# Splitting the gate weights of a forgetting attention in quarters, at fixed places of two engines' order

## The chip, the core and the metric

The kernel runs on one core of a Trainium2 chip. The core has five engines that each work through their own list of instructions in order and wait for each other by semaphores: TensorE (PE in the profile; PEld is its loading of weights), VectorE (DVE), ScalarE (ACT), GpSimd (POOL) and SyncE (SP), which only issues DMAs here. The metric is the device time of one launch in microseconds (us).

## The reference

One DeepNorm layer over a sequence of 1024 frames with 1024 channels, in float32: a forgetting attention with 16 heads of 64, then a SwiGLU with 2816 channels. Both are modulated by a conditioning vector. What matters here is the attention with its output gate:

```python
def fox_mixer(h, w_in, b_f, q_g, k_g, w_o):
    proj = h @ w_in
    q, k, v, f_logit, o = jnp.split(proj, [D, 2 * D, 3 * D, 3 * D + N_HEADS], axis=-1)
    ...
    y = fox_block_attention(q, k, v, F)     # causal softmax(q k^T * scale + F_q - F_k) v, per head
    y = y.transpose(0, 2, 1, 3).reshape(B, T, D)
    return (y * jax.nn.sigmoid(o)) @ w_o
```

The gate `o` is one more projection of `h`, 1024 columns wide.

## The kernel before

Float32 products are made from high and low parts: an operand x is cast on ScalarE to a rounded type (`xh`), VectorE subtracts that from x (`xl`), and TensorE sums `xh*yh + xl*yh + xh*yl`. The kernel first projects q, k and v for all frames and stores them in DRAM, then runs the attention head by head, then the output projection and the SwiGLU.

The attention works in pairs of heads (`pr`, 8 of them). For a head, `scores` makes the products of q and k (L535, L536; tile `s`) in six steps into two PSUM buffers of two banks each. VectorE adds the causal mask to the diagonal block (L540) and takes the row maximum (L542, `nm`), ScalarE makes the exponential (L543, `p`). A buffer is free again once its exponential has been made. `values` transposes `p` on TensorE (L596, `t`), casts it (L601, `ph`), subtracts (L602, `pl`) and multiplies it with the values (L579, L580; `o`). At the end of a half of the rows, ScalarE copies one half of `o` (L585, `yt`) and VectorE adds the other (L586, `y`). GpSimd multiplies `y` by the gate and the inverse row sums (`lb`, from a small DRAM round trip): `sg` (L636), then `lb*sg` (L657) and `y*lb` (L659), the last as soon as `y` is there.

`gates` is a generator that fills TensorE's stream: for each pair and each half of the rows it makes 24 products (8 blocks of the contraction, 3 products each, L631, bank `og`), and the tanh (L635) after the 24th. `GC` says how many of these products each of the 12 steps of a head takes. Their weights are 128 columns for a pair. `gate_raw` loads them (512 KB, tile `wor`, one buffer), and `gate_weights` splits them in two parts of 4 blocks each: a cast of 512 elements a partition (L614, `woh`) and a subtraction (L615, `wol`). Part 0 of the next pair is made while the current pair's second half runs, at its block 5, right after the load is issued; part 1 is made when the next pair begins. The same buffer `wor` takes the first weights of the output projection (`wo100r`) after the last pair.

The kernel is written through a tile layer that lists instructions in program order and then reorders each engine's list, by what it expects to be ready. `tc.keep_in_program_order(i)` holds instruction i behind everything that was written before it on its engine. The kernel before uses it only in the SwiGLU. Heads are written one step ahead: all scores of head 0 come first, then 12 steps, each with some gate products, a step of the next head's scores, and a step of this head's values.

Of the kernel before, what the change touches and what calls it, by code (L numbers as in the profile page):

```python
# [9 lines left out]
F32R = mybir.dt.float32r  # L10
BF16 = mybir.dt.bfloat16
AF = mybir.ActivationFunctionType
ALU = mybir.AluOpType
# [3 lines left out]
P = 128  # L17
# [7 lines left out]
NP = H // 2  # L25
# [10 lines left out]
def f32(ap):  # L36
    return ap.bitcast(F32)
# [8 lines left out]
def fox_trunk_kernel(  # L46
# [17 lines left out]
    nc = tc.nc  # L64
# [3 lines left out]
    wo = fox_w_o[0]  # L68
# [28 lines left out]
    def bank(tag, name):  # L97
        return ps.tile([P, 512], F32, name=name, tag=tag, bufs=3 if tag == "T" else 1)
# [150 lines left out]
    for kt in range(KT):  # L249
# [9 lines left out]
        wh, wl = w0[kt // 2]  # L259
# [227 lines left out]
    gws = {}  # L487

    def gate_raw(pr):
        raw = ld[0].tile([P, KT, P], F32, name=f"wor{pr}", tag="owr", bufs=1)  # L490
        nc.sync.dma_start(raw, win[:, 3 * D + H + pr * P:3 * D + H + (pr + 1) * P]
                          .rearrange("(k p) e -> p k e", p=P))
        gws[pr] = [raw]
# [19 lines left out]
    pv_cm.__exit__(None, None, None)  # L513
    wt_cm.__exit__(None, None, None)


    yp = ctx.enter_context(tc.tile_pool(name="yp", bufs=1, side="right", reuse_waits="tile"))
    y32 = yp.tile([P, NP, T], F32, name="y32")
# [2 lines left out]
    def right(name):  # L521
        cm = tc.tile_pool(name=name, bufs=1, side="right", reuse_waits="tile")
        at_cms.append(cm)
        return cm.__enter__()

    a_o, ld1, a_p, a_t, at = [right(f"at_{n}") for n in "olptx"]
# [79 lines left out]
                wait.append((product, (hf, kbk, c0, ph, pl)))  # L606
                yield

    def gate_weights(pr, part):

        raw = gws[pr][0][:, part * 4:part * 4 + 4, :]
        wh = a_o.tile([P, 4, P], F32R, name=f"woh{pr}{part}", tag=f"owh{part}", bufs=1)
        wl = a_o.tile([P, 4, P], F32R, name=f"wol{pr}{part}", tag=f"owl{part}", bufs=1)
        nc.scalar.copy(wh, raw)  # L614
        nc.vector.tensor_tensor(wl, raw, f32(wh), ALU.subtract)  # L615
        gws[pr].append((wh, wl))

    def gates():

        gate_weights(0, 0)  # L620
        for pr in range(NP):
            gate_weights(pr, 1)
            for hf in HALVES:
                a = bank("T", f"og{pr}_{hf}")
                for kt in range(KT):
                    if hf == HB and kt == 5 and pr + 1 < NP:
                        gate_raw(pr + 1)
                        gate_weights(pr + 1, 0)
                    wh, wl = gws[pr][1 + kt // 4]
                    for n, (l, r) in enumerate(((wh, hTh), (wl, hTh), (wh, hTl))):  # L630
                        nc.tensor.matmul(a, l[:, kt % 4, :], r[hf][:, kt, :], start=(kt == 0 and n == 0),  # L631
                                         stop=(kt == KT - 1 and n == 2))
                        if kt == KT - 1 and n == 2:
                            sg = at.tile([P, 512], F32, name=f"sg{pr}_{hf}", tag="sg", bufs=2)
                            nc.scalar.activation(sg, a, AF.Tanh, scale=0.5)  # L635
                            nc.gpsimd.tensor_scalar(sg, sg, 0.5, 0.5, op0=ALU.mult, op1=ALU.add)  # L636
                            sgs[pr, hf] = sg
                        yield
# [24 lines left out]
    HA, HB = HALVES  # L663
# [35 lines left out]
    def start(h):  # L699
# [4 lines left out]
        return tl, probs, scores(h, tl, state[pr][0], probs)  # L704

    sgs, gg = {}, gates()
    cur, wait = start(0), []
    run(cur[2], 12)
    for h in range(H):
        pr = h // 2  # L710
        nxt = start(h + 1) if h + 1 < H else None
        v = values(h, cur[0], cur[1])
        for step in range(12):
            if h % 2 and step in (1, 5):
                hf = HALVES[step == 5]
# [162 lines left out]
    for hf in HALVES:  # L878
# [8 lines left out]
        for cc in range(4):  # L887
# [5 lines left out]
            for i in range(4):  # L893
                tt = hf * 4 + i
                a = out_bank(i, f"wa{tt}_{cc}")[:, 0:256]
                for kt in range(KT):
                    wh, wl = w[kt // 4]
# [75 lines left out]
        return others  # L973

    banks, fds = {}, []
    keep = tc.keep_in_program_order

    def open_bank(tag, ff, n):
        banks[tag, ff] = psA.tile([P, 512], F32, name=f"{tag}{ff}", tag=tag, bufs=n)
# [324 lines left out]
```

## Time and profile before

| what | us |
|---|---|
| median of 3 runs | 1408.03 (1404.87 to 1409.60) |
| the profiled execution | 1409.46, its span 1407.7 |
| TensorE busy | 1354.5 (96%) |
| VectorE busy | 1025.7 (73%) |
| ScalarE busy | 584.6 (42%) |
| GpSimd busy | 343.5 (24%) |
| attention, first score product to last value product | 342.7 to about 649 |

The span runs from the first to the last instruction. A busy time is the union of an engine's instructions; matmuls are pipelined, so two that follow each other overlap in the rows, and the distance of their starts is what one costs. PEclk is TensorE's granted clock as a share of its full 2.4 GHz. A note in brackets at the end of a row is the time in which the engine sat idle before it, and the instruction that ended this. The mean granted clock of this execution was 0.992.

### The profile page before, as it was taken

What the parts mean: (1) busy time and instruction counts of PE and PEld (TensorE: products, weight loads), DVE (VectorE), ACT (ScalarE), POOL (GpSimd) and SP (SyncE); (2) the same over time, 40 slices, a digit from 0 to 9 for tenths busy, and PEclk for the clock granted to TensorE, in tenths of its full rate; (3) what the DMA queues carried; (4) which work ended last, traced back from release to release, by engine and by line L of the source; (5) the groups of instructions that cost most, each with busy time, mean ns of one, the idle gap of its engine ahead of it and who ended that gap; (6) DMA issues with size and microseconds to landing.
All of it is one profiled execution on the core that took longest, in us unless ns stands there. A gap on an engine that the chain in (4) does not pass through costs nothing.

```text
span 1407.7 us, 19137 instructions
## 1 busy us (share of the span) xinstructions
PE 1354.5 (96%) x6832; PEld 1133.2 (81%) x6832; DVE 1025.7 (73%) x1636; ACT 584.6 (42%) x1025; POOL 343.5 (24%) x250
## 2 busy tenths in 40 slices
PE   5899999999999999999999899999999999999997
PEld 4678778887888888888998777888888888788886
DVE  6765486663888888888767766667767667685897
ACT  3532232222776777676245522333333334543320
POOL 2443003210111111114000265444445431000011
PEclk9899999999999999999999999999999999999999
DMA  9748765658566565546636334555655556987531
GB/s 277 201 150 264 246 198 159 206 187 223 128 149 152 137 143 132 136 106 215 191 120 194 98 112 142 174 171 183 198 180 173 176 200 237 367 293 223 195 118 75
DMA packets 212305, 254.41 MB, mean 181 GB/s; under 512 B 13353, under 2 KB 138609, under 8 KB 212210
## 3 DMA queue, kind: packets, MB, share of 16 engines
q1 hardware_dynamic: 211058, 251.09, 59.0%
q10 hardware_dynamic: 1152, 2.10, 0.4%
q8 instruction: 54, 0.88, 0.3%
q14 instruction: 41, 0.34, 0.1%
HBM read 185.18 MB, written 67.96 MB: 180 GB/s over the span
## 4 chain that ended last, share of the span: by engine, by line
PE 71%; DVE 13%; DMA 5%; POOL 4%; issue 3%; ACT 2%; SPq 1%; POOLq 0%; DVEq 0%; ACTq 0%
PE og L631 5%; PE y L1222 4%; PE y L1224 4%; PE y L1223 4%; PE B L1073 4%; PE B L1074 4%; PE B L1075 4%; PE t L596 4%; PE A L1073 3%; PE A L1075 3%; PE A L1074 3%; PE D L1073 3%; PE D L1075 3%; PE D L1074 3%; PE s L535 2%
## 5 line engine op out<-in xcount | busy, mean ns | idle before, releaser
L1222 PE MATMUL y<-ring 128*128 128x512 f32 (+1 forms) x319 | 122.6, 385 | 2.8 <-ACT fpu L1181 2.8
L1223 PE MATMUL y<-ring 128*128 128x512 f32 (+1 forms) x319 | 122.6, 384 | 0.0
L1224 PE MATMUL y<-ring 128*128 128x512 f32 (+1 forms) x319 | 122.1, 385 | 0.0
L1030 DVE TENSOR_TENSOR ring<-r,ring 128x1024 fp32r<-128x1024 f32 x77 | 95.0, 1248 | 36.1 <-ACT ring L1029 35.5
L1029 ACT CAST ring<-r 128x1024 fp32r<-128x1024 f32 x77 | 80.4, 1053 | 95.7 <-PE y L1224 51.0
L602 DVE TENSOR_TENSOR pl<-t,ph 128x512 fp32r<-128x512 f32 x192 | 103.7, 548 | 14.8 <-ACT ph L601 13.4
L844 ACT CAST slots<-wi 128x512 fp32r<-128x512 f32 x88 | 54.3, 621 | 140.4 <-PE D L1074 68.9
L543 ACT ACTIVATE p<-s,nm 128x640 f32<-128x640 f32 (+7 forms) x128 | 95.4, 746 | 39.0 <-DVE nm L542 38.6
L1073 PE MATMUL B<-XT,slots 128*128 128x512 f32 x264 | 104.7, 396 | 6.0 <-DVE fd L1088 4.8
L601 ACT CAST ph<-t 128x512 fp32r<-128x512 f32 x192 | 90.9, 479 | 44.4 <-PE t L596 41.9
L1074 PE MATMUL B<-XT,slots 128*128 128x512 f32 x264 | 103.5, 392 | 0.0
L1075 PE MATMUL B<-XT,slots 128*128 128x512 f32 x264 | 103.4, 392 | 0.0
L542 DVE TENSOR_REDUCE nm<-s 128x1 f32<-128x640 f32 (+7 forms) x128 | 95.5, 748 | 2.5
L596 PE MATMUL t<-ident,p 128*128 128x128 f32 x576 | 95.6, 273 | 0.6 <-DVE pl L602 0.4
L845 DVE TENSOR_TENSOR slots<-wi,slots 128x512 fp32r<-128x512 f32 x88 | 71.6, 813 | 25.0 <-ACT slots L844 25.0
L596 PEld LDWEIGHTS t<-ident,p 128*128 128x128 f32 x576 | 71.2, 141 | 11.5 <-DVE pl L602 2.2
L579 PE MATMUL o<-ph,va 128*128 128x512 f32 x192 | 76.6, 399 | 0.0
L1222 PEld LDWEIGHTS y<-ring 128*128 128x128 f32 x319 | 60.3, 189 | 16.0 <-ACT fpu L1181 3.2
L535 PE MATMUL s<-ka,qa 128*128 128x320 f32 (+2 forms) x192 | 67.5, 352 | 4.8 <-ACT p L543 4.7
L1224 PEld LDWEIGHTS y<-ring 128*128 128x128 f32 x319 | 60.5, 190 | 11.9
L1223 PEld LDWEIGHTS y<-ring 128*128 128x128 f32 x319 | 60.3, 189 | 11.6
L1073 PE MATMUL A<-h2h,slots 128*128 128x512 f32 x176 | 69.1, 392 | 0.0
(571 smaller groups left out, 3744.4 us busy)
## 6 DMA issues: line engine op xcount, KB each, us to landing
wi<-in_ffn_w_in_dram SPq DMA_DIRECT2D x50, 512.0 KB
aw<-in_ada_w_dram SPq DMA_DIRECT2D x46, 512.0 KB
r<-sd SPq DMA_DIRECT2D x77, 256.0 KB
sd<-hs SPq DMA_DIRECT2D x44, 256.0 KB
r<-td SPq DMA_DIRECT2D x44, 256.0 KB
sd<-fd SPq DMA_DIRECT2D x33, 256.0 KB
r<-in_ffn_w_out_dram SPq DMA_DIRECT2D x33, 256.0 KB
qa<-qs SPq DMA_DIRECT2D x32, 256.0 KB
```

Source lines behind the costliest of these rows:

```text
L535: nc.tensor.matmul(o, qa[:, q], ka[:, c0:c0 + w], start=True, stop=False)
L542: nc.vector.tensor_reduce(nm, view, axis=axis, op=ALU.max, negate=True)
L543: nc.scalar.activation(pv, view, AF.Exp, bias=nm, accum_out=lcs[hf][:, s * 4 + jj:s * 4 + jj + 1])
L596: nc.tensor.transpose(tb[:, jj * P:(jj + 1) * P], probs[hf * 4 + jj][:, kbk * P:(kbk + 1) * P], ident)
L602: nc.vector.tensor_tensor(pl[:, c0:], tb[:, c0:], f32(ph[:, c0:]), ALU.subtract)
L1030: nc.vector.tensor_tensor(t[:, 1], raw, f32(t[:, 0]), ALU.subtract)
L1073: nc.tensor.matmul(b, hi, rh, start=(first and k == 0), stop=False, skip_group_check=True)
L1074: nc.tensor.matmul(b, hi, rl, start=False, stop=False, skip_group_check=True)
L1075: nc.tensor.matmul(b, lo, rh, start=False, stop=(k == 3), skip_group_check=True)
L1222: nc.tensor.matmul(b[:, c0:c1], sh, wh, start=first, stop=False, skip_group_check=True)
L1223: nc.tensor.matmul(b[:, c0:c1], sh, wl, start=False, stop=False, skip_group_check=True)
L1224: nc.tensor.matmul(b[:, c0:c1], sl, wh, start=False, stop=last, skip_group_check=True)
```

## The change

`gate_weights` now makes half a part at a time (256 elements a partition): a pair's weights are four quarters instead of two halves, each with its own cast and subtraction, and each held in program order. The quarters of a pair's second part stand at blocks 0 and 1 of its first half of the rows; those of the next pair's first part at blocks 5 and 7 of the second half. The load of the next pair's raw block is issued at block 2 instead of block 5. The tiles' sizes and the products are unchanged.

```diff
--- before.py
+++ after.py
@@ -513,6 +513,8 @@
     pv_cm.__exit__(None, None, None)
     wt_cm.__exit__(None, None, None)
 
+    keep = tc.keep_in_program_order
+
 
     yp = ctx.enter_context(tc.tile_pool(name="yp", bufs=1, side="right", reuse_waits="tile"))
     y32 = yp.tile([P, NP, T], F32, name="y32")
@@ -606,26 +608,30 @@
                 wait.append((product, (hf, kbk, c0, ph, pl)))
                 yield
 
-    def gate_weights(pr, part):
-
-        raw = gws[pr][0][:, part * 4:part * 4 + 4, :]
-        wh = a_o.tile([P, 4, P], F32R, name=f"woh{pr}{part}", tag=f"owh{part}", bufs=1)
-        wl = a_o.tile([P, 4, P], F32R, name=f"wol{pr}{part}", tag=f"owl{part}", bufs=1)
-        nc.scalar.copy(wh, raw)
-        nc.vector.tensor_tensor(wl, raw, f32(wh), ALU.subtract)
-        gws[pr].append((wh, wl))
+    def gate_weights(pr, part, half):
+
+        if half == 0:
+            gws[pr].append([a_o.tile([P, 4, P], F32R, name=f"wo{n}{pr}{part}", tag=f"ow{n}{part}", bufs=1)
+                            for n in "hl"])
+        raw = gws[pr][0][:, part * 4 + half * 2:part * 4 + half * 2 + 2, :]
+        wh, wl = [t[:, half * 2:half * 2 + 2, :] for t in gws[pr][1 + part]]
+        keep(nc.scalar.copy(wh, raw))
+        keep(nc.vector.tensor_tensor(wl, raw, f32(wh), ALU.subtract))
 
     def gates():
 
-        gate_weights(0, 0)
+        for half in range(2):
+            gate_weights(0, 0, half)
         for pr in range(NP):
-            gate_weights(pr, 1)
             for hf in HALVES:
                 a = bank("T", f"og{pr}_{hf}")
                 for kt in range(KT):
-                    if hf == HB and kt == 5 and pr + 1 < NP:
+                    if hf == HA and kt < 2:
+                        gate_weights(pr, 1, kt)
+                    if hf == HB and kt == 2 and pr + 1 < NP:
                         gate_raw(pr + 1)
-                        gate_weights(pr + 1, 0)
+                    if hf == HB and kt in (5, 7) and pr + 1 < NP:
+                        gate_weights(pr + 1, 0, kt == 7)
                     wh, wl = gws[pr][1 + kt // 4]
                     for n, (l, r) in enumerate(((wh, hTh), (wl, hTh), (wh, hTl))):
                         nc.tensor.matmul(a, l[:, kt % 4, :], r[hf][:, kt, :], start=(kt == 0 and n == 0),
@@ -973,7 +979,6 @@
         return others
 
     banks, fds = {}, []
-    keep = tc.keep_in_program_order
 
     def open_bank(tag, ff, n):
         banks[tag, ff] = psA.tile([P, 512], F32, name=f"{tag}{ff}", tag=tag, bufs=n)
```

The first place is TensorE's order at the start of the attention, where head 0 has its scores made: the last three of eleven gate products that stand between its scores `s_5` and `s_6` (`s` are score tiles, `og_1` is the first gate bank, `woh` and `wol` its weights). Before:

```order
L631 MATMUL og_1_2885<-hTl_114,woh_2877 128x512
L631 MATMUL og_1_2885<-hTh_113,woh_2877 128x512
L631 MATMUL og_1_2885<-hTh_113,wol_2878 128x512
L535 MATMUL s_6_2815<-ka_2431,qa_2430 128x448
L536 MATMUL s_6_2815<-kb_2433,qb_2432 128x448
```

Now `s_6` follows `s_5` at once, and so on through head 0's scores; the first gate product and the first transposes (`t`) stand here, behind the first half of the scores `s_5` of head 1:

```order
L537 MATMUL s_5_2924<-ka_2864,qa_2863 128x384
L538 MATMUL s_5_2924<-kb_2866,qb_2865 128x384
L637 MATMUL og_1_2883<-hTh_113,woh_2877 128x512
L598 MATMUL t_1_0_2894<-ident,p_4_2796 128x128
L598 MATMUL t_1_0_2894<-ident,p_5_2806 128x128
L637 MATMUL og_1_2883<-hTh_113,wol_2878 128x512
L598 MATMUL t_1_0_2894<-ident,p_6_2816 128x128
```

24 gate products, 16 transposes and 3 products with the values, which stood ahead of these scores of head 1, now stand behind them.

The second place is ScalarE's order at the same time; `vt` are casts of the projection, `p` the exponentials of head 0 (L543 before, L545 now). Before:

```order
L324 CAST vt_2695<-v1acc_2670 128x4x2x64
L614 CAST woh_2877<-wor_2444 128x512
L614 CAST woh_2881<-wor_2444 128x512
L324 CAST vt_2738<-v1acc_2713 128x4x2x64
L324 CAST vt_2767<-v1acc_2742 128x4x2x64
L543 ACTIVATE p_4_2796,lc_1_2793<-s_4_2795,nm_4_2802 128x640
L543 ACTIVATE p_5_2806,lc_1_2793<-s_5_2805,nm_5_2812 128x768
L543 ACTIVATE p_6_2816,lc_1_2793<-s_6_2815,nm_6_2822 128x896
```

Now:

```order
L545 ACTIVATE p_0_2836,lc_0_2794<-s_0_2835,nm_0_2842 128x128
L545 ACTIVATE p_0_2836,lc_0_2794<-s_0_2835,nm_1_2846 128x256
L545 ACTIVATE p_2_2850,lc_0_2794<-s_2_2849,nm_2_2856 128x384
L545 ACTIVATE p_2_2850,lc_0_2794<-s_2_2849,nm_3_2860 128x512
L618 CAST woh_2877<-wor_2444 128x256 x2
L618 CAST woh_2884<-wor_2444 128x256
L545 ACTIVATE p_4_2891,lc_1_2793<-s_4_2890,nm_4_2907 128x640
```

The casts of the gate weights have moved from among the projection's casts to behind the last exponential of head 0.

The third place is VectorE's order at the seam between the first two pairs, from the sum `y` of the last head's first half of the rows on (L586 before, L588 now). `nm` are maxima, `pl` the low parts of the transposed `p`, and `wol` the gate weights' subtraction, 512 wide before and 256 now. Before:

```order
L586 TENSOR_TENSOR y_2777<-o_1_3198,yt_1_3323 64x512
L540 TENSOR_TENSOR s_0_3279<-s_0_3279,maskb 128x128
L542 TENSOR_REDUCE nm_1_3310<-s_0_3279 128x1
L602 TENSOR_TENSOR pl_0_2_3341<-t_0_2_3337,ph_0_2_3340 128x256
L540 TENSOR_TENSOR s_2_3333<-s_2_3333,maskb 128x128
L542 TENSOR_REDUCE nm_2_3352<-s_2_3333 128x1
L602 TENSOR_TENSOR pl_0_3_3362<-t_0_3_3359,ph_0_3_3361 128x128
L615 TENSOR_TENSOR wol_3385<-wor_3295,woh_3384 128x512
L540 TENSOR_TENSOR s_2_3333<-s_2_3333,maskb 128x128
L542 TENSOR_REDUCE nm_3_3356<-s_2_3333 128x1
```

Now, from one row earlier:

```order
L542 TENSOR_TENSOR s_0_3285<-s_0_3285,maskb 128x128
L588 TENSOR_TENSOR y_2777<-o_1_3202,yt_1_3327 64x512
L544 TENSOR_REDUCE nm_1_3314<-s_0_3285 128x1
L619 TENSOR_TENSOR wol_3302<-wor_3207,woh_3301 128x256
L604 TENSOR_TENSOR pl_0_2_3347<-t_0_2_3343,ph_0_2_3346 128x256
L542 TENSOR_TENSOR s_2_3339<-s_2_3339,maskb 128x128
L544 TENSOR_REDUCE nm_2_3358<-s_2_3339 128x1
L604 TENSOR_TENSOR pl_0_3_3368<-t_0_3_3365,ph_0_3_3367 128x128
L619 TENSOR_TENSOR wol_3392<-wor_3207,woh_3391 128x256
L542 TENSOR_TENSOR s_2_3339<-s_2_3339,maskb 128x128
L544 TENSOR_REDUCE nm_3_3362<-s_2_3339 128x1
```

One `wol` of 256 has come between `nm_1` and `pl_0_2`, and the one of 512 behind `pl_0_3` is one of 256; the other two quarters stand ahead of `pl_0_1` and behind the other `y`, outside this piece.

## Rows read from the trace of the kernel before

**Rows 1.** The page: busy time by engine, and the chain by engine.

```profile
PE 1354.5 (96%) x6832; PEld 1133.2 (81%) x6832; DVE 1025.7 (73%) x1636; ACT 584.6 (42%) x1025; POOL 343.5 (24%) x250
...
PE 71%; DVE 13%; DMA 5%; POOL 4%; issue 3%; ACT 2%; SPq 1%; POOLq 0%; DVEq 0%; ACTq 0%
```

**Rows 2.** What TensorE waited for, 340 to 650 us: total, times, longest.

```profile
PE s L535 <- ACT p L543: 4.7, 9, 0.6
```

**Rows 3.** Timeline of TensorE at a seam: start, us, engine, line, tiles, shape.

```profile
389.41 0.40 PE L631 MATMUL og<-hTl,woh 128*128 128x512 f32 x1
390.34 0.45 PE L535 MATMUL s<-ka,qa 128*128 128x384 f32 x1 [0.54 <-ACT p L543]
```

**Rows 4.** Timeline of TensorE, start of the attention.

```profile
343.99 0.40 PE L631 MATMUL og<-hTh,woh 128*128 128x512 f32 x1
...
346.52 0.37 PE L535 MATMUL s<-ka,qa 128*128 128x448 f32 x1
...
354.94 0.66 PE L596 MATMUL t<-ident,p 128*128 128x128 f32 x4
355.35 0.49 PE L580 MATMUL o<-pl,va 128*128 128x512 f32 x1
355.67 0.40 PE L579 MATMUL o<-ph,va 128*128 128x512 f32 x1
...
356.95 0.44 PE L535 MATMUL s<-ka,qa 128*128 128x384 f32 x1 [0.44 <-ACT p L543]
```

**Rows 5.** Timeline of TensorE, later in the first pair.

```profile
365.19 0.33 PE L596 MATMUL t<-ident,p 128*128 128x128 f32 x1 [0.26 <-DVE pl L602]
365.83 0.44 PE L535 MATMUL s<-ka,qa 128*128 128x384 f32 x1 [0.31 <-ACT p L543]
```

**Rows 6.** Timeline of VectorE at the first seam.

```profile
383.93 0.69 DVE L586 TENSOR_TENSOR y<-o,yt 64x512 f32<-64x512 f32 x1
...
384.99 0.42 DVE L542 TENSOR_REDUCE nm<-s 128x1 f32<-128x256 f32 x1
385.33 0.41 DVE L602 TENSOR_TENSOR pl<-t,ph 128x256 fp32r<-128x256 f32 x1
...
386.85 1.69 DVE L615 TENSOR_TENSOR wol<-wor,woh 128x512 fp32r<-128x512 f32 x1
...
388.79 0.69 DVE L542 TENSOR_REDUCE nm<-s 128x1 f32<-128x512 f32 x1
```

**Rows 7.** Timeline of GpSimd at the first seam.

```profile
384.76 1.29 POOL L659 TENSOR_TENSOR y<-y,lb 128x512 f32<-128x512 f32 x1 [4.33 <-DVE y L586]
386.02 0.62 POOL L636 TENSOR_SCALAR sg<-sg 128x512 f32<-128x512 f32 x1
386.72 1.28 POOL L657 TENSOR_TENSOR lb<-lb,sg 128x512 f32<-128x512 f32 x1
```

**Rows 8.** Line 615, 340 to 660 us: ns min/median/max, first and last start.

```profile
L615 DVE TENSOR_TENSOR wol<-wor,woh x14: 679/1168/1694, 381.5 to 614.8; 128x512 fp32r<-128x512 f32 x14
```

**Rows 9.** Timeline of ScalarE at the first seam.

```profile
386.18 0.64 ACT L614 CAST woh<-wor 128x512 fp32r<-128x512 f32 x1
```

**Rows 10.** Timelines of VectorE and ScalarE, last softmax steps of head 0.

```profile
355.19 1.41 DVE L542 TENSOR_REDUCE nm<-s 128x1 f32<-128x512 f32 x2
...
356.11 0.69 ACT L543 ACTIVATE p<-s,nm 128x512 f32<-128x512 f32 x1
```

**Rows 11.** Windows: stretch, us, TensorE busy (count), granted clock, DMA share, GB/s.

```profile
661.00:665.00 4.00, 2.33 (x17) 1.00 0.39 111
343.99:356.95 12.96, 12.45 (x64) 1.00 0.82 195
386.30:424.30 38.00, 37.46 (x220) 1.00 0.60 141
```

**Rows 12.** Windows around a fall of the clock in the prologue.

```profile
142.00:145.00 3.00, 0.52 (x3) 1.00 0.16 59
145.00:149.00 4.00, 4.00 (x11) 0.57 0.91 274
```

## The prediction

> **What bounds the kernel now.** I read the page first. TensorE is busy for 96% of the span and the chain of waits lies on it for 71% [rows 1], so a cast or a subtraction that moves costs something only where TensorE then waits for it, and only TensorE's own gaps can be won back. The list of what TensorE waited for in the attention comes second: 4.7 us in nine waits, all of them a score product waiting for the exponential that frees its PSUM bank [rows 2]. Third comes the timeline of one seam between two head pairs. The last gate product before it starts at 389.41 and the score product behind it at 390.34 [rows 3]. That is 0.93 us where 0.23 would do (eleven gate products start in the 2.53 us from 343.99 to 346.52 [rows 4]): 0.70 us lost. One such wait lies at each of the seven seams between the eight pairs. The other two lie in the first pair: 0.44 at 356.95 [rows 4] and 0.31 at 365.83 [rows 5].
>
> VectorE and GpSimd show why [rows 6, 7]. VectorE's subtraction for the weights' low half (L615) takes 1.69 us at 386.85, where the same shape takes 0.68 elsewhere [rows 8]. GpSimd's product of lb and sg runs from 386.72 to 388.00 beside it, and the subtraction ends 0.55 after that: it has stood still while GpSimd read. The maximum nm behind it starts at 388.79, the exponential waits for that, and the bank for the exponential. VectorE's other work in that time, which reads PSUM, keeps its usual length.
>
> A rule of the Trainium skill speaks against this change. The page "SBUF — State Buffer", section "Who interferes with whom", says that a VectorE instruction with both inputs in SBUF contends with a GpSimd instruction that reads SBUF, and that the second to issue waits out the first. The 0.55 us above agrees with it. By that rule a subtraction of half the width is not safe either: it pays whatever is left of the GpSimd instruction. The sum below can be had from [rows 6, 7] alone.
>
> **The raw blocks, three steps sooner.** The cast at 386.18 follows its predecessor without idle time [rows 9], and the view of its line shows no wait for the load. I cost this at nothing; the casts stay where ScalarE's order puts them. If the load were late, it would show as idle time in front of those casts.
>
> **The start of the attention.** This is the first cost. Before, both of pair 0's casts stand among those of the last projection, and the 24 gate products of its first bank, split 11, 6, 4 and 3 among the scores of head 0, fill the time in which TensorE would wait for softmax [rows 4]. Now the casts are held behind what was written ahead of them, which includes all eight exponentials of head 0, as ScalarE's order shows. In TensorE's new order no gate product and no transpose stands before the second matmul of s_5 of head 1. The scores come when softmax frees their banks, nearly as before; what stood between them is left over. That is 24 gate products at 0.23 (5.5 us), 16 transposes at 0.41 for four (354.94 to 355.35: 1.6 us) and 3 products with the values at 0.24 to 0.32 (0.8): 7.9 us [rows 4].
>
> Some of it comes back. ScalarE and VectorE no longer put casts and subtractions of head 0 between the last two exponentials, so nm starts near 354.9 instead of 355.19 and the exponential near 355.6 instead of 356.11 [rows 10]: s_5 of head 1 restarts 0.5 us sooner. The left-over gate products then fill the waits later in the pair: 0.26 and 0.31 us of idle at 365 [rows 5], and by the starts nearly as much again around them, about 1.0 together. Net 6.4 us, between 5.5 (the transposes and value products are absorbed too, and nothing else) and 7.9 (nothing comes back). TensorE has no slack to repay it: over a whole pair it is busy for 37.46 of 38.00 us [rows 11].
>
> **The clock.** From 343.99 to 356.95 TensorE is busy for 12.45 us at the full level of 2.4 GHz [rows 11]. Without the filler only the five score groups are left, about 4 us of work, with waits of up to 2.5 us (343.99 to 346.52 [rows 4]) ahead of each. What that does to the granted clock no row shows for this place. The nearest one: after 3 us with 0.52 busy, the clock was 0.57 on average over the next 4 us, thus mostly at the lower level of 1.2 GHz, though TensorE was busy throughout [rows 12]. Against it, 4 us with 2.33 busy kept the full level [rows 11]. My stretch lies nearer the first. A stretch of some 3.4 us at half speed (0.57 over 4 us) costs 1.7 us if TensorE has work for all of it, and little if it falls among the waits. I take 2.0, from 0 (no fall) to 3.5 (two falls, both under full work).
>
> "TensorE: Matmul & The Clock Gate", section "What's actually happening", in the Trainium skill says the same in general: the lower clock is the default and activity lifts it. The trace agrees [rows 12].
>
> **The seams.** Here the change is to win, at most 0.70 to 0.75 us at each of seven, 5.2 in all. I follow VectorE's new order with the times of the seam at 386. The first half stands between nm_0 and pl_0_1, and its cast on ScalarE stands ahead of ph_0_1 and of the copy yt: these move by 0.3 (half of a cast's 0.64 [rows 9]), and y starts near 384.2 instead of 383.93. GpSimd follows y's end by 0.14 [rows 6, 7]: its product runs from 385.05 to 386.34. The second half stands behind y and nm_1, so it starts near 385.25, inside that product, and ends near 386.6 instead of 385.6: a collision that the kernel before does not have. Then pl_0_2, a mask, nm_2 and pl_0_3 take 1.4 us as before (385.33 to the subtraction at 386.85, less 0.1 that it waits for its cast). The third half comes at 387.95, while GpSimd does sg and then lb from 387.07 to 388.35; it ends near 388.65. A mask later nm_3 starts at 388.9, against 388.79 [rows 6]. Three short subtractions have met two GpSimd instructions, where one long one met one. The fourth half, behind the other y, comes 0.1 ahead of GpSimd and costs TensorE nothing.
>
> So a seam is worth between -0.75 us (no half meets GpSimd) and +0.6 (sg is itself pushed back by the second half, and each half also waits 0.1 to 0.2 for its cast). By the rows I have +0.1, by the waits for the casts somewhat more; I take +0.3, 2.1 us for seven. Two more casts and two more subtractions in each pair cost ScalarE and VectorE some 0.1 us of overhead apiece; they hide under TensorE's work.
>
> The last pair's second half of the weights now ends some 4 us later, and with it the load of wo100r into the same buffer. Its cast stands three rows later on ScalarE, so I add nothing; a late load would add up to 1 us, once.
>
> **Sum.** 6.4 + 2.0 + 2.1 = 10.5 us on an execution of 1409.46 us (span 1407.7): 1420.0. That execution lies 1.4 above the median of 1408.03, so 1418.5 from there. I forecast 1419, with 1414 to 1422 as this case's own range.
>
> **Rivals.**
> - Not slower, because the seams heal. Place: the seven seams; price: -0.75 each, -5.2. It needs the second and third halves to end before GpSimd's products begin, or to run beside them, and a clock that does not fall: 6.4 - 5.2 = +1.2, 1410. For it: a subtraction without GpSimd takes 0.68 even at full width [rows 8]. Against it: y itself starts GpSimd, 0.14 later, and nm_1 of 0.42 stands between y and the half. It decides at a gap ahead of the seam's score product of under 0.2 us.
> - The seams heal, but the clock falls: 6.4 + 2.0 - 5.2 = +3.2, 1412.
> - Everything near its upper end: 7.0 at the start, 3.5 for the clock, 0.57 at each seam (4.0): +14.5, 1423. For it: the halves hold ScalarE up as well, which my walk through VectorE's order counts only in part.
> - The change doesn't do what it says, since the loads were never late: true for the loads, and it adds nothing to the sum.
> - Faster: the seams heal and over 5 us of the start come back. For the latter TensorE would need gaps in pair 0, and the waits list has under 1 us there [rows 2].
>
> **Chances.** Forecast 0.60, upper case 0.18, seams healed with a falling clock 0.06, not slower 0.13, faster 0.03. 0.3% is 4.2 us, about what a measurement of this kernel can tell from no change. The first two are slower, as is half of the third: 0.81. The rest of the third and the fourth are the same: 0.16. Faster: 0.03. The range of 8 in 10 runs from 1411, inside the not-slower cases, to 1424.
>
> **What would show it.** Right: in the changed trace TensorE's busy share between the first score and 13 us later falls under half, the first gate product stands near 357, and the granted clock drops to half for a few us at 347 to 361. At the seams the second half of a pair's subtractions takes 1.2 to 1.5 us instead of 0.4, and the wait for the exponential stays at 0.6 to 1.1. The first gate product of pair 1 comes 6 to 9 us later than 386.30. Wrong: halves of 0.4 us throughout and no wait at the seams (then the third term is -5.2), or a first bank of gate products that starts well before head 1's scores.

## The result, and the profile after

The changed kernel took 1423.53 us (median of 4 runs, 1418.35 to 1427.72), the kernel before 1408.43 beside it (4 runs, 1404.87 to 1409.60). The ratio is 1.0107, 95% interval 1.0083 to 1.0132: slower by about 15 us, where 1419 was forecast. The profiled execution of after took 1421.59 us, 12.1 more than the profiled one of before.

The page of after, the lines that answer to [rows 1]: busy time by engine, and the chain of waits by engine.

```profile
PE 1357.8 (96%) x6832; PEld 1134.1 (80%) x6832; DVE 1031.7 (73%) x1652; ACT 586.8 (41%) x1041; POOL 345.2 (24%) x250
...
PE 71%; DVE 12%; DMA 4%; POOL 4%; ACT 4%; issue 3%; SPq 1%; POOLq 0%; DVEq 0%; ACTq 0%
```

Little of the loss is seen here: the shares are within two points of those of before, and TensorE's busy time is 3.3 us longer for the same 6832 matmuls. So I cut the run into stages, each from the start of its first matmul, which the timelines give for both kernels.

| stage | before, us | after, us | difference |
|---|---|---|---|
| start of the span to the first score | 342.68 | 342.56 | -0.12 |
| first score to pair 1's first gate product | 43.62 | 54.20 | +10.58 |
| pair 1's to pair 7's first gate product (six pairs) | 227.84 | 231.46 | +3.62 |
| pair 7's first gate product to the output projection | 35.49 | 36.01 | +0.52 |
| all that comes behind | 758.02 | 755.57 | -2.45 |

The sum is 12.15, the difference of the two spans. The last row is work that TensorE does in nearly the same order in both. In before it holds 3.4 us at half clock that after's profiled execution doesn't have. The window of before (stretch, us, TensorE busy and count, granted clock, DMA share, GB/s):

```profile
800.90:804.30 3.40, 3.40 (x9) 0.50 0.48 144
```

TensorE is busy throughout, so that is worth 1.7. Another 0.7 is one wait behind the attention, of a transpose for a cast on ScalarE (tile `h32b`): 1.8 in before, 1.1 in after. Both lie in work that the change doesn't touch. The attention itself lost 14.7.

**The start.** What TensorE waited for in the attention of after, 340 to 665 us (total, times, longest), answers to [rows 2], 4.7 in nine:

```profile
PE s L537 <- ACT p L545: 11.4, 11, 2.2
PE t L598 <- DVE pl L604: 1.4, 7, 0.2
PE o L581 <- DVE y L588: 0.2, 1, 0.2
```

The second row had two waits in before, both in the first pair:

```profile
PE t L596 <- DVE pl L602: 0.4, 2, 0.3
```

TensorE's timeline at the start of the attention, which answers to [rows 4]. In brackets is the idle time ahead of a row and what ended it:

```profile
342.56 0.30 PE L537 MATMUL s<-ka,qa 128*128 128x320 f32 x1
...
346.22 0.74 PE L537 MATMUL s<-ka,qa 128*128 128x448 f32 x1 [2.20 <-ACT p L545]
...
348.74 0.63 PE L537 MATMUL s<-ka,qa 128*128 128x512 f32 x1
349.16 0.63 PE L538 MATMUL s<-kb,qb 68*128 68x512 f32 x1
350.86 0.47 PE L537 MATMUL s<-ka,qa 128*128 128x128 f32 x1 [1.07 <-ACT p L545]
...
352.81 0.69 PE L537 MATMUL s<-ka,qa 128*128 128x384 f32 x1 [0.72 <-ACT p L545]
...
358.45 0.69 PE L537 MATMUL s<-ka,qa 128*128 128x384 f32 x1 [2.20 <-ACT p L545]
...
359.25 0.63 PE L637 MATMUL og<-hTh,woh 128*128 128x512 f32 x1
359.68 0.63 PE L598 MATMUL t<-ident,p 128*128 128x128 f32 x2
```

The first gate product starts at 359.25, where before it stood at 343.99, and nothing fills the four waits ahead of it. Two matmuls of 512 columns start 0.42 apart (348.74, 349.16), where before eleven took 0.23 each [rows 4]: TensorE runs at half speed. The windows of after say for how long; the last is the pair of heads behind the first, from one first gate product to the next, and answers to the last of [rows 11]:

```profile
342.56:355.56 13.00, 8.86 (x28) 0.63 0.46 119
346.00:363.00 17.00, 12.64 (x35) 0.50 0.70 157
...
359.25:363.00 3.75, 3.75 (x14) 0.50 0.96 196
...
363.00:366.00 3.00, 3.00 (x19) 1.00 0.16 23
...
396.76:435.30 38.54, 37.61 (x220) 1.00 0.61 139
```

From 345.9 to 363.0 the clock is at the lower of its two levels, 1.2 GHz, where before it was full [rows 11]. It fell during the first wait of 2.20 and came back after TensorE had run from 358.45 without a wait.

**The seams.** VectorE's timeline of after at the first seam, which answers to [rows 6]:

```profile
395.07 0.69 DVE L588 TENSOR_TENSOR y<-o,yt 64x512 f32<-64x512 f32 x1 [0.20 <-ACT yt L587]
395.80 0.42 DVE L544 TENSOR_REDUCE nm<-s 128x1 f32<-128x256 f32 x1
396.25 1.22 DVE L619 TENSOR_TENSOR wol<-wor,woh 128x256 fp32r<-128x256 f32 x1
397.40 0.41 DVE L604 TENSOR_TENSOR pl<-t,ph 128x256 fp32r<-128x256 f32 x1
...
398.72 0.88 DVE L619 TENSOR_TENSOR wol<-wor,woh 128x256 fp32r<-128x256 f32 x1
...
399.84 0.69 DVE L544 TENSOR_REDUCE nm<-s 128x1 f32<-128x512 f32 x1
...
403.55 0.42 DVE L619 TENSOR_TENSOR wol<-wor,woh 128x256 fp32r<-128x256 f32 x1
```

GpSimd beside it, as in [rows 7]:

```profile
395.90 1.30 POOL L665 TENSOR_TENSOR y<-y,lb 128x512 f32<-128x512 f32 x1 [6.47 <-DVE y L588]
397.16 0.79 POOL L642 TENSOR_SCALAR sg<-sg 128x512 f32<-128x512 f32 x1
398.04 1.28 POOL L663 TENSOR_TENSOR lb<-lb,sg 128x512 f32<-128x512 f32 x1
403.66 1.47 POOL L665 TENSOR_TENSOR y<-y,lb 128x512 f32<-128x512 f32 x1 [4.34 <-DVE y L588]
```

And TensorE, as in [rows 3]:

```profile
397.37 0.31 PE L538 MATMUL s<-kb,qb 68*128 68x320 f32 x1
397.86 0.66 PE L598 MATMUL t<-ident,p 128*128 128x128 f32 x4 [0.19 <-DVE pl L604]
...
400.27 0.39 PE L637 MATMUL og<-hTl,woh 128*128 128x512 f32 x1
401.40 0.45 PE L537 MATMUL s<-ka,qa 128*128 128x384 f32 x1 [0.74 <-ACT p L545]
```

Read the three together. The second quarter starts at 396.25 inside GpSimd's product (395.90 to 397.20) and ends 0.27 after it: 1.22 us. The third starts at 398.72 inside the next one (398.04 to 399.32) and ends 0.28 after it: 0.88. It is the same at all seven seams: 1.22 to 1.24 for the second quarter, 0.88 for the third. The fourth, at 403.55, comes 0.11 ahead of GpSimd, keeps its 0.42, and now GpSimd's product takes 1.47 instead of 1.3. The maximum at 399.84 comes late, and the score product starts 1.13 behind the last gate product, where 0.23 would do: 0.90 lost, 0.70 before. A second, smaller gap is new: the second quarter holds up pl, and a transpose waits 0.19 for it; it starts 0.49 behind the score product ahead of it, where 0.15 does elsewhere, so 0.34 is lost there. The two make 0.54 more than before, of the 0.60 that a pair lost.

The chain of waits of after from 396 to 402 us (start, us, what) shows what this seam hangs on:

```profile
396.25 1.22 DVE wol L619
397.47 0.33 DVE pl L604
...
398.80 0.80 DVE wol L619
...
399.84 0.70 DVE nm L544
...
401.15 0.20 ACT p L545
401.36 0.04 issue
401.40 0.45 PE s L537
```

Over the attention, the line of the subtractions (ns min/median/max, first and last start) answers to [rows 8]:

```profile
L619 DVE TENSOR_TENSOR wol<-wor,woh x32: 415/427/1235, 358.7 to 635.0; 128x256 fp32r<-128x256 f32 x32
```

### The profile page after: what moved, and what is told of

It reads as the page before. It is cut to its first block, busy times and chain, and to the rows that moved or that the text cites. A ratio compares the mean times of both kernels' runs of the same rounds, so it can differ in the third digit from the quotient of the medians.

```text
span 1419.8 us, 19173 instructions
## 1 busy us (share of the span) xinstructions
PE 1357.8 (96%) x6832; PEld 1134.1 (80%) x6832; DVE 1031.7 (73%) x1652; ACT 586.8 (41%) x1041; POOL 345.2 (24%) x250
## 4 chain that ended last, share of the span: by engine, by line
PE 71%; DVE 12%; DMA 4%; POOL 4%; ACT 4%; issue 3%; SPq 1%; POOLq 0%; DVEq 0%; ACTq 0%
PE y L1227 5%; PE y L1229 5%; PE y L1228 5%; PE og L637 4%; PE B L1078 4%; PE B L1079 4%; PE B L1080 4%; PE t L598 4%; PE A L1078 3%; PE A L1080 3%; PE A L1079 3%; PE D L1078 3%; PE D L1079 3%; PE D L1080 3%; PE s L537 2%
## 5 line engine op out<-in xcount | busy, mean ns | idle before, releaser
L545 ACT ACTIVATE p<-s,nm 128x640 f32<-128x640 f32 (+7 forms) x128 | 95.5, 746 | 43.9 <-DVE nm L544 43.8
```

What stands on the lines that cost most here:

```text
L545: nc.scalar.activation(pv, view, AF.Exp, bias=nm, accum_out=lcs[hf][:, s * 4 + jj:s * 4 + jj + 1])
```

## The experiments

**Which part of the change costs the first pair.** `pair0_free` is after, with pair 0's quarters free of the hold:

```diff
-        keep(nc.scalar.copy(wh, raw))
-        keep(nc.vector.tensor_tensor(wl, raw, f32(wh), ALU.subtract))
+        hold = keep if pr else (lambda i: i)
+        hold(nc.scalar.copy(wh, raw))
+        hold(nc.vector.tensor_tensor(wl, raw, f32(wh), ALU.subtract))
```

> The changed kernel, with the hold in program order taken off pair 0's quarters only. Theory (two places: the start of the attention costs about 10.5 us in the profiled execution, 6.4 of lost filler and the rest clock; the seven seams cost about 0.56 each): the start is as before, first gate product near 344, pair 1's first gate product within 0.5 us of 386.3, clock at the full level throughout the attention; the seams stay as in the changed kernel, a wait of 0.7 each and 38.5 us from pair to pair. In all +4 us against the kernel before, 1412. Rival (twice as many casts and subtractions slow the whole attention, the places matter little): most of the 12 to 15 us stays, 1418 or more.

Measured: 1411.01 us (10 runs), ratio 1.0026 (1.0014 to 1.0038). The stretch from the first score to pair 1's first gate product is 43.64, as before, at full clock throughout:

```profile
339.80:383.44 43.64, 42.52 (x239) 1.00 0.61 146
```

`pair0_held` is the opposite: before, with the hold on pair 0's two halves alone (the same edit in before's `gate_weights`, with `keep` for pair 0 only).

> The kernel before, unsplit, with its old load place, where only pair 0's two casts and two subtractions are held in program order. Theory: the start alone, +8 to +11 us (1417 to 1420); first gate product near 359, granted clock at half from about 346 for 10 us or more; from pair to pair 37.95 us as before, with a wait of 0.55 at each seam. Rival (the number of quarters): within 1 us of the kernel before.

Measured: 1417.46 (4 runs), ratio 1.0074 (1.0049 to 1.0098). The stretch is 54.31, and the clock lies at half from 345.6 for 17.1 us, as in after; a later pair takes 37.95, where before took 37.97. So the first cost is the hold on pair 0 alone, whole or quartered, early load or late.

**The clock's share of it.** `filled` is after with products that no one reads put among head 0's scores, to keep TensorE at work there:

```diff
-    run(cur[2], 12)
+    def fill(n, name):
+        b = bank("T", name)
+        for i in range(n):
+            keep(nc.tensor.matmul(b, hTh[HA][:, i % KT, 0:P], hTh[HA][:, i % KT, :], start=True, stop=True))
+
+    for n, w in ((4, 8), (4, 6), (2, 4), (2, 2)):
+        run(cur[2], n)
+        fill(w, f"fill{n}{w}")
```

> The changed kernel with 20 gate-sized products on TensorE, whose result nobody reads, put in the waits among head 0's scores (8, 6, 4 and 2 of them, as long as the waits there in the kernel before's timeline). Theory (a part of the start's loss is the clock): the granted clock stays at the full level from 343 to 357 or falls later and for less time; pair 1's first gate product comes 3 to 4 us sooner than in the changed kernel, near 393, and the time falls by as much, to about 1419. Rival (all of the start's loss is work displaced, the clock falls over waits that cost nothing): pair 1's first gate product stays at 396 to 397 and the time at 1422 to 1425.

Measured: 1421.56 (4 runs), ratio 1.0105 (1.0080 to 1.0129); the stretch took 53.04, only 1.16 less than in after. A miss as an experiment: the wait of 2.20 us ahead of head 1's s_5 was left open, and the clock fell in it and stayed low over the work that followed. The window of `filled`:

```profile
352.80:359.60 6.80, 5.98 (x19) 0.50 0.79 162
```

`filled_full` closes that wait too: the last filler has 10 products instead of 2.

> After, with 28 products whose results nothing reads put among head 0's scores, eight of them more than in the first such kernel, all eight ahead of head 1's first score, so that the wait of 2.20 us ahead of head 1's second score tile is filled too; TensorE's order behind them is the same. From the first score to pair 1's first gate product before took 43.62, after 54.20, and the first such kernel 53.04, of which 6.8 us at half clock. Theory (10.6 is about 6.5 for work that no longer fills waits and about 4 for the clock): no half-clock stretch stands at the start of the attention, and that stretch takes about 50. Rival (the clock costs little, all is lost filling): about 53 to 54, whatever the clock does. Should the half clock stand there all the same, the run tells nothing on this. The time follows the stage less well, since the order of the last layers' matmuls differs: 1416 to 1421.

Measured: 1419.15 (4 runs), ratio 1.0076 (1.0049 to 1.0102). The windows of `filled_full`, first score to first gate product, and from there to pair 1's first, and the row of TensorE that holds the longest wait left, head 1's s_5:

```profile
339.41:353.70 14.29, 12.84 (x60) 1.00 0.63 155
353.70:389.47 35.77, 35.77 (x209) 1.00 0.47 116
```

```profile
353.24 0.44 PE L537 MATMUL s<-ka,qa 128*128 128x384 f32 x1 [0.77 <-ACT p L545]
```

Full clock, and 50.06 in all. So the loss of 10.58 splits in 6.44 for gate products, transposes and value products that no longer fill waits (50.06 - 43.62), and 4.14 for the clock (54.20 - 50.06): 2.40 ahead of the first gate product (16.69 in after against 14.29) and 1.74 behind it (37.51 against 35.77). The 6.44 has two parts: s_5 of head 1 comes 13.83 behind the first score (353.24) where before needed 14.27 (356.95), so 0.44 is won, and from there to pair 1's first gate product it takes 36.23 instead of 29.35, so 6.88 is lost.

**The quarters themselves, and the load.** `no_hold` is after without any `keep` in `gate_weights`: quarters and the early load alone.

> The changed kernel with no hold at all: quarters and the early load stay, the tile layer orders them. Theory: no lost filler, pair 1's first gate product within 1 us of 386.3; at the seams it hangs on where the quarters land beside GpSimd's products, between -0.5 and +0.6 us each: 1405 to 1413, the same as before within 0.3%. Rival (number of quarters or the early load): 1415 or more.

Measured: 1409.27 (10 runs), ratio 1.0010 (0.9994 to 1.0026): the same. A pair takes 37.93. The quarters cost nothing where the order is free. VectorE's timeline says why: at the seam the free order puts the third and the fourth quarter next to each other, in the place where before has its one subtraction of 1.69 us [rows 6].

```profile
387.27 1.84 DVE L619 TENSOR_TENSOR wol<-wor,woh 128x256 fp32r<-128x256 f32 x2
```

So this run shows no cost of the number of quarters or of the early load; it doesn't show that four separate places would be free.

`load_late` is after with the raw block's load back at block 5 (`kt == 5` for `kt == 2`).

> The changed kernel with the raw blocks' load back at block 5. Theory (the sooner load gives nothing): the same as the changed kernel within the scatter of its runs (1418 to 1428), no wait of a cast for its load. Rival (the sooner load matters): casts wait for the load ahead of the seam and the time rises by over 3 us, or falls by as much if the sooner load is in the way.

Measured: 1421.83 (4 runs), ratio 1.0099 (1.0075 to 1.0123); a pair takes 38.57, after's 38.58. The casts of the quarters behind pair 0's first three, in `load_late`; the view of that line shows no idle time of ScalarE ahead of them:

```profile
L618 ACT CAST woh<-wor x29: 403/407/419, 360.1 to 631.1; 128x256 fp32r<-128x256 f32 x29
```

The load was never late; three steps sooner win and cost nothing that shows.

**The seams.** `pool_sub` is before with the subtraction on GpSimd, so that the two engines can't collide over it:

```diff
-        nc.vector.tensor_tensor(wl, raw, f32(wh), ALU.subtract)
+        nc.gpsimd.tensor_tensor(wl, raw, f32(wh), ALU.subtract)
```

> The kernel before with one word changed: the weights' subtraction runs on GpSimd instead of VectorE, unsplit and not held. Theory (the seam's wait is VectorE's subtraction standing still while GpSimd reads SBUF): no subtraction is left on VectorE to stand still, the wait of 0.55 at the seams goes, 37.2 us from pair to pair instead of 37.95, in all -4 to -5 us, 1403 to 1404. Rival (the wait is the softmax chain of that place itself, the subtraction only fills it): the wait stays and the time is that of the kernel before.

Measured: 1406.18 (12 runs), ratio 0.9987 (0.9973 to 1.0001), not clearly different from before. A pair takes 37.32 instead of 37.97, and no wait of TensorE is left from pair 1 to pair 7. But 2.6 us come back at the end of the attention: the last raw block's buffer is free later, and with it the load of wo100r into its place, which is issued 3.65 behind pair 7's first gate product instead of 2.30. VectorE's timeline of `pool_sub` there, and TensorE's:

```profile
615.98 1.23 DVE L684 TENSOR_TENSOR wo100l<-wo100r,wo100h 128x1024 fp32r<-128x1024 f32 x1 [2.15 <-ACT wo100h L683]
```

```profile
618.73 0.55 PE L596 MATMUL t<-ident,p 128*128 128x128 f32 x3 [2.13 <-DVE pl L602]
```

VectorE waits 2.15 for the cast of that block, pl stands behind it, and TensorE waits 2.13 for pl; then the clock is at 0.51 for 3.4 us.

`before_nogate` and `after_nogate` leave the other partner out: GpSimd's two products of the gate (lb by sg, y by that) cover 8 columns instead of 512.

```diff
-        nc.gpsimd.tensor_tensor(lbs[hf], lbs[hf], sgs[pr, hf], ALU.mult)
         y = y32[:, pr, hf * 512:(hf + 1) * 512]
-        nc.gpsimd.tensor_tensor(y, y, lbs[hf], ALU.mult)
+        nc.gpsimd.tensor_tensor(lbs[hf][:, 0:8], lbs[hf][:, 0:8], sgs[pr, hf][:, 0:8], ALU.mult)
+        nc.gpsimd.tensor_tensor(y[:, 0:8], y[:, 0:8], lbs[hf][:, 0:8], ALU.mult)
```

> The kernel before, with the same cut of GpSimd's two gate products to 8 columns. Theory: the subtraction at the seam takes 0.68 instead of 1.66, the wait of 0.55 goes, pair to pair 37.2 us: -4 to -5 us, 1404. Rival: the wait stays, within 1 us of the kernel before.

> The changed kernel, with GpSimd's two products of the gate cut from 512 columns to 8: the attention's output is not gated beyond them. Theory: the second and third quarters take 0.42 us at every seam instead of 1.22 and 0.88, the wait there goes, pair to pair falls from 38.55 to 37.1 to 37.5 us: -8 to -10 us against the changed kernel, 1414. The start is unchanged, first gate product near 359. Rival (the longer order on VectorE and ScalarE makes the wait): it stays near 0.7, pair to pair 38.3 or more.

Measured: before_nogate 1400.93 (5 runs), ratio 0.9942 (0.9918 to 0.9965), 37.13 a pair; after_nogate 1414.67 (10 runs), ratio 1.0048 (1.0033 to 1.0062), 37.58 a pair. Not one quarter is longer than 427 ns in `after_nogate`:

```profile
L619 DVE TENSOR_TENSOR wol<-wor,woh x32: 412/425/427, 353.5 to 623.0; 128x256 fp32r<-128x256 f32 x32
```

So GpSimd stretches them, and its two products are worth 1.00 of after's 38.58 a pair. But they are worth 0.84 of before's 37.97 as well. Of the 0.60 that the change adds to a pair, 0.45 is left without them (37.58 against 37.13), slightly more than I had expected: either the quarters on VectorE at their bare length, or the casts at fixed places on ScalarE.

`quarters_pool` tells these apart: after with pair 0 free, the casts held in the other pairs as in after, and the subtractions on GpSimd.

```diff
-        keep(nc.scalar.copy(wh, raw))
-        keep(nc.vector.tensor_tensor(wl, raw, f32(wh), ALU.subtract))
+        hold = keep if pr else (lambda i: i)
+        hold(nc.scalar.copy(wh, raw))
+        eng = nc.vector if (pr, part) == (NP - 1, 1) else nc.gpsimd
+        eng.tensor_tensor(wl, raw, f32(wh), ALU.subtract)
```

> After, with pair 0 free of the hold, the casts of the quarters on ScalarE at their fixed places as in after, and their subtractions on GpSimd (of the last pair's second block on VectorE). A middle pair took 37.97 us before, 38.54 in after with pair 0 free, 37.32 in before with the subtractions on GpSimd. Theory (what a pair lost is the quarters on VectorE, stretched by GpSimd's product, in front of head scores): about 37.3 per pair, and a time of 1403 to 1405. Rival (the four fixed places on ScalarE cost as much: with GpSimd's products cut to nothing a pair still took 0.45 more than before with the same cut): 37.7 to 38.0 per pair, 1406 to 1409.

Measured: 1403.89 (12 runs), ratio 0.9976 (0.9961 to 0.9991); 37.32 a pair, to the digit that of `pool_sub`. In these pairs the casts at fixed places on ScalarE cost nothing that shows; what the pairs lost is VectorE's: by the two runs with 8 columns 0.45 for four quarters at fixed places without any collision, and, if the two add up, only the other 0.15 for meeting GpSimd twice instead of once. Behind pair 7's first gate product, though, this run takes 35.92, more than before's 35.49: the fourth quarter's place holds the last raw block, the load of wo100r is issued 6.10 behind that product, VectorE waits 0.35 for its cast, and a transpose 0.74 for the pl behind that.

**A better version.** `pool_most` is before with the subtractions on GpSimd, all but the last pair's second one, so that its raw block comes free as early as before.

```diff
-        nc.vector.tensor_tensor(wl, raw, f32(wh), ALU.subtract)
+        eng = nc.vector if (pr, part) == (NP - 1, 1) else nc.gpsimd
+        eng.tensor_tensor(wl, raw, f32(wh), ALU.subtract)
```

> Before, with the subtractions of the gates' weights on GpSimd, but the last pair's second one left on VectorE, where it was. In the kernel with all sixteen on GpSimd the six middle pairs took 37.32 us each (before 37.97), and the stretch from pair 7's first gate product to the first product with wa took 38.13 (before 35.49), with a wait of 2.1 behind the load into the raw block's place and 3.4 us at half clock behind it. Theory (the late subtraction of the last pair keeps the raw block's place and so delays that load): the wait and the half clock go, the pairs stay at 37.3, the stretch comes back to 35.5 to 36, and the time is 1403 to 1404. Rival (the load is late for another reason, GpSimd's other work of the last pair): 38 stays in that stretch and the time is 1406 as with all sixteen.

Measured: 1403.31 (6 runs), ratio 0.9955 (0.9938 to 0.9973): faster than before. A pair takes 37.34, and the stretch from pair 7's first gate product to the output projection 34.88, where `pool_sub` took 38.13. TensorE's waits from 335 to 665 us in `pool_most`, against [rows 2]:

```profile
PE wa L171 <- DVE wo110l L685: 1.0, 1, 1.0
PE s L535 <- ACT p L543: 0.8, 2, 0.4
PE wa L171 <- DVE wo111l L685: 0.7, 1, 0.7
PE t L596 <- DVE pl L602: 0.5, 2, 0.3
```

The two waits of a score product that are left are those in the first pair. The two on wa lie behind the attention and stand in before too. The subtractions of `pool_most` on GpSimd take longer than on VectorE alone, and in that list no wait is theirs:

```profile
L616 POOL TENSOR_TENSOR wol<-wor,woh x13: 1278/1284/1288, 379.6 to 602.4; 128x512 fp32r<-128x512 f32 x13
```

## Why the prediction was right, and where its sizes were off

Slower was given 0.81, and the range of 8 in 10, 1411 to 1424, held 1423.53 with 0.5 us to spare; two of the four runs lie above it. The forecast's own range, 1414 to 1422, did not hold it: what came is the rival with everything near its upper end (1423, +14.5, given 0.18), by its size though not by the reason given for it, that the quarters hold ScalarE up. So the mechanisms were right in the main, two of the three sizes were about half of what came, and that the range still held is partly luck. Term by term:

- **Work that fills no wait any more: right.** 6.4 predicted, 6.44 measured at full clock (`filled_full`), and due to the hold on pair 0 alone (`pair0_free`, `pair0_held`). Its parts held too: 0.5 was to be won ahead of head 1's s_5 and 0.44 was; of the 7.9 left over about 1.0 was to fill later waits, and 6.88 was lost there, which leaves 1.0.
- **The clock: the mis-sized term.** 2.0 predicted, at most 3.5; measured 4.14. I took the length of the low stretch, 3.4 us, from a fall in the prologue behind which TensorE had unbroken work [rows 12]. Here waits of 1.07, 0.72 and 2.20 followed the first, and the clock stayed at 0.50 for 17.1 us. I had said that a low clock costs little where it falls among waits; but 2.40 of the 4.14 lie there, since the score products at half speed start the next softmax later.
- **The seams: predicted at half their size.** 2.1 for seven predicted; measured 3.62 for six pairs and 0.52 behind, 4.1, the upper end given (0.6 each). The walk through VectorE's order held in its times: from y's start, the second quarter was to end at 2.4 us and ended at 2.40 (395.07 to 397.47); nm_3 was to start at 4.7 and started at 4.77. What I left out is the other reader of that order: the stretched second quarter also delays pl, and a transpose waits (0.19 at 397.86, 7 such waits in the attention). And two more subtractions were to cost VectorE some 0.1 us and to hide under TensorE's work. They cost 0.17 apiece (four of 0.425 against two of 0.68), the casts did hide (`quarters_pool`), and the subtractions at their fixed places did not: with GpSimd's products gone the quarters still cost 0.45 a pair. So the second collision is the smaller part of what the change added to a pair.
- **The load: right**, nothing (`load_late`). The last pair's later load of wo100r (issued 7.26 behind pair 7's first gate product instead of 2.30): nothing that shows, its cast follows its predecessor without idle time; the 0.52 at the end is about what a seam costs elsewhere (0.60).
- **Sum.** 10.5 predicted for the attention, 14.7 measured: 0.0 from the first term, 2.1 from the clock, 2.0 from the seams. The profiled execution was 2.45 shorter behind the attention, and 1.9 below its median.

By the signs named beforehand: the second quarter took 1.22 (1.2 to 1.5 named) and the waits 0.74 (0.6 to 1.1). The first gate product came at 359.25, not near 357, pair 1's 10.46 later and not 6 to 9, both by the clock. "Busy share under half in the first 13 us" was a bad sign: it was 8.86 of 13.00, because half speed makes the same work look about twice as busy.

The rival that ends on the other side, seams that heal, asked for a gap under 0.2 us: it was 0.74. `pool_sub` shows that 0.65 a pair was to be had there from another engine. Whether another place on VectorE would have given it is not shown; the free order did not (`no_hold`, 37.93).

The rule on the second to issue, in the Trainium skill's "SBUF — State Buffer", "Who interferes with whom", agrees with the rows in both directions: VectorE second, 1.22 and 0.88 instead of 0.42; GpSimd second, 1.47 instead of 1.3.

## What to carry to other kernels

Before holding an instruction in program order, look up what the free order had put ahead of it: here two casts among the last projection's let 24 products fill softmax waits, and the hold cost that filler and then the clock. Halving an instruction that is stretched by another engine doesn't halve the stretch: each half pays for what it meets, and where the engine's order is tight the additional places cost something without any collision, so move the work to the engine it collides with, if that one has time, and check whose buffer it then frees late. When pricing a low clock, count all the waits behind the first one, not the length of another stretch.

## What was not expected of the hardware

- The clock stayed at half for 17.1 us though TensorE was busy for 12.64 of 17.00 us, with waits of at most 2.20 in between. With the waits filled (`filled_full`, the longest left 0.77) it stayed full; with one of 2.20 left open (`filled`), it fell for 6.8 us, over work with hardly a wait.
- A stretched instruction seems to pass the delay on: GpSimd's next instruction (sg, 397.16) started while VectorE's stretched second quarter still ran (396.25 to 397.47) and took 0.79 instead of 0.62 [rows 7]; at all seven seams it was 0.79 to 0.80. That it waited for the quarter is inferred from these times.
- The same subtraction of 128 by 512 takes 1.28 us on GpSimd and 0.68 on VectorE alone, but up to 1.69 there beside GpSimd [rows 8]; where only VectorE is waited for, the slower engine is the faster place.
